# First RMSNorm of a decoder layer: sums of squares from a second, token-major load of x, and three weight tiles projected before the norm is known

## The chip, the core and the metric

The kernel runs on one core of a Trainium2 chip. A core has five engines with queues of their own: TensorE (PE, matmuls; PEld is its weight load), VectorE (DVE), ScalarE (ACT), GpSimd (POOL) and SyncE (SP, which here only issues DMAs and reads registers). The metric is the device time of one execution in microseconds (us), smaller is better. Of the kernel before there are three timed runs: 2433.55, 2440.73 and 2443.16 us, median 2440.73.

## The reference

One decoder layer with a hybrid mixer, for 512 prompt tokens and 32 sample tokens (8 sequences of 4) that share all weights, in float32. What matters here is its beginning:

```
def rmsnorm(x, w):
    y = x * rsqrt(mean(x * x, axis=-1) + EPS)       # mean over D_MODEL = 2048
    return y * w

h = rmsnorm(x, norm_mix_w)
proj = h @ w_in                                      # columns: q, k, v, z, xbc, dt_raw
xbc_c = silu(causal_dwconv(xbc, ...));  dt = softplus(dt_raw + dt_bias)
... attention, Mamba-2 scan, output projection, second norm, gated MLP, last norm
```

A token's factor rsqrt(...) multiplies a whole row of h, so it can be left out of the projection and multiplied into its result: proj = (x * w) @ w_in, times the factor of each token. Both kernels do that.

## The kernel before

**Layout.** Activations lie with features in partitions and tokens along the row: x comes as `xT`, 16 blocks (k = 0 to 15) of 128 features by 544 tokens, the tokens in two halves of 272 (256 prompt, 16 sample). Each float32 operand is split in two parts of lower precision, hi = rounded, lo = rest, and a product is three matmuls (hi x hi, hi x lo, lo x hi; `mm3`, L166). The split of weights is `wload` (L137): a DMA into `wraw`, ScalarE writes `whi` (L150), VectorE writes `wlo` (L151). An output tile of 128 columns of w_in is 2 halves x 16 k x 3 = 96 matmuls of 272 columns.

**First stage (L239 to L282).** For each k one DMA brings `xt`; `xh` is made by VectorE for even k (L251) and by ScalarE for odd k (L253), `xl` by VectorE (L254), times the norm's gain. ScalarE squares `xt` (L257, L260), and the squares are added up, three by VectorE, the others by GpSimd (L261), into `ssq`, which is a sum over k with features still in partitions. At the same time the weights of the first two output tiles (`FIRST`: columns 8 and 10 of the xbc part) come in pieces of 256 columns, and TensorE runs the 192 matmuls of both tiles as x arrives (L276). Amid them, after k = 13, `rms_rstd` (L207) sums `ssq` over the partitions with a matmul against ones (`pn`), which also spreads the sum over all partitions; ScalarE takes the square root (L213) and VectorE the reciprocal (L214) of 128 x 272 values for each half. The result is `rstd`.

**What follows.** The pool sA (`xt`, the first tiles' weights, the squares) is released and the pool sS takes its memory: what is first written in sS waits for the last reader in sA. `dt_linear` (L336) runs 64 matmuls for the columns of dt into PSUM (`podt`) with the weights `wdthi` (L274, L275). Then the tiles of xbc follow, each by `xbc` (L326): the matmuls of `linear`, then an evacuation that multiplies PSUM by `rstd` into `pre` (L305, L306), a convolution in `acc` (one ScalarE pass L314 and three VectorE passes L316), and a SiLU by ScalarE (L318, L319). The two first tiles have their matmuls behind them already, and go straight to the evacuation.

**What sets the order.** TensorE runs in the order in which the code is written. Small jobs (`dt_stage`, `lam`, `ssd`) are generators, which are polled between matmuls by a modelled clock (`side`), so that their matmuls are put between those of the tiles: `dt_stage` multiplies `podt` by `rstd` into `dtr` on VectorE (L347 to L349) and then transposes it by five small matmuls `pd` (L355). The order on the other engines is the scheduler's, by priority; it is fixed when the program is built, and each engine runs it in line.

**SP.** Its queue issues the loads of x and weights. After the first tile's weights 32 reads of the page table into registers stand in it (L631), ahead of all later weight loads. Three buffers hold `whi` and `wlo`, two hold `wraw`.

Of the kernel before, what the change touches and what calls it, by code (L numbers as in the profile page):

```python
# [16 lines left out]
P = 128  # L17
# [82 lines left out]
def body(tc, i, o):  # L100
# [12 lines left out]
    def rd(t):  # L113
        return t.bitcast(F32)
# [122 lines left out]
    fw = [[], []]  # L237
    sub = 256
    for k in range(NK):  # L239
        xt = sA.tile([P, 2, HT], F32, name="xt", tag="xt", bufs=6)  # L240
        dma(out=xt, in_=i["xT"][k])
        if k % 8 == 0:
            ch = [wload(i["w_in"][32 + j][:, k * P:k * P + WCH], sub, sA) for j in FIRST]
            for f in range(2):
                fw[f].append(ch[f][:2])
        if k % 2 == 0:
            for c in ch:
                c[2]((k % 8) // 2)
        xs[k] = xslot(k)
        if k % 2 == 0:  # L250
            V.tensor_scalar(xs[k][0], xt, nw_mix[:, k:k + 1], None, op0=ALU.mult)  # L251
        else:
            A.activation(xs[k][0], xt, AF.Copy, scale=nw_mix[:, k:k + 1])  # L253
        V.scalar_tensor_tensor(xs[k][1], xt, nw_mix[:, k:k + 1], rd(xs[k][0]), op0=ALU.mult, op1=ALU.subtract)  # L254
        e, acc = (V, ssq2) if k % 4 == 2 else (G, ssq)
        if k in (0, 2):
            A.activation(acc, xt, AF.Square)  # L257
        else:
            sq = sA.tile([P, 2, HT], F32, name="sq", tag="sq", bufs=3)
            A.activation(sq, xt, AF.Square)  # L260
            e.tensor_tensor(acc, acc, sq, op=ALU.add)  # L261
    k1 = pack(cst, "k1")
    ones, nw_ffn, nw_fin = (k1[n] for n in ("ones", "nw_ffn", "nw_fin"))
    V.tensor_tensor(ssq, ssq, ssq2, op=ALU.add)
    kS = pack(sC, "kS")
# [6 lines left out]
    wdt = kS["w_dt"].rearrange("p (k h) -> p k h", h=SH)  # L272
    whi = sC.tile([P, NK, 2 * SH], FR, name="wdthi")
    A.activation(whi[:, :, 0:SH], wdt, AF.Copy)  # L274
    V.tensor_tensor(whi[:, :, SH:2 * SH], wdt, rd(whi)[:, :, 0:SH], op=ALU.subtract)  # L275
    for k in range(NK):  # L276
        for f in range(2):
            for hf in range(2):
                mm3(first[f][hf], kslice(fw[f], k), xs[k], hf, k == 0, k == NK - 1)
        if k == 13:  # L280
            rstd = rms_rstd(cst, ssq, DM, tag="rstd")
    sA.release()  # L282
# [1150 lines left out]
def host_inputs(x):  # L1433
# [132 lines left out]
```

## Time and profile before

| | us |
|---|---|
| median of three runs | 2440.73 |
| the profiled execution's own time | 2442.75 |
| its span, first to last instruction | 2441.0 |
| TensorE busy | 2355.5 (96%) |
| VectorE busy | 2083.3 (85%) |
| ScalarE busy | 1141.7 (47%) |
| GpSimd busy | 722.6 (30%) |

The span and the own time differ by what lies before the first and after the last instruction. TensorE's clock has two levels, 1.2 and 2.4 GHz; the profile gives the granted share of the upper one, 0.986 as a mean of this execution. In the page's chain of waits 59% of the span is TensorE's. Times in rows count from the start of the span.

### The profile page before, as it was taken

The numbers are of one execution on the slowest core, as the hardware profiler recorded it, in microseconds if no ns is written. First come the engines' busy times: TensorE is split into PE (matmuls) and PEld (weight loads), VectorE is DVE, ScalarE is ACT, GpSimd is POOL, SyncE is SP. The second block draws the span as 40 slices with busy tenths as digits, with TensorE's granted clock in tenths as the row PEclk, the third lists the DMA queues.
The fourth block names the chain that finished last, engine by engine and source line by source line (L and its number), as shares of the span: only waits on it lengthen the run. The fifth ranks groups of instructions, "written<-read, shape, count | busy, mean of one in ns | idle before, by whom it ended". The sixth has DMA issues, their size and how long they took to land.

```text
span 2441.0 us, 46377 instructions
## 1 busy us (share of the span) xinstructions
PE 2355.5 (96%) x18184; PEld 2302.7 (94%) x18184; DVE 2083.3 (85%) x2893; ACT 1141.7 (47%) x1651; POOL 722.6 (30%) x655
## 2 busy tenths in 40 slices
PE   8999999999999999899999999999999899899997
PEld 7989898998999999899999999999999899898997
DVE  8686778787877556999999999999999988989986
ACT  5645345656565323444444444444444534435345
POOL 4243233333321113522222222322221222423223
PEclk9999999999999999899999999999999999999999
DMA  5434444444555443243434343333433755747432
GB/s 163 130 126 129 157 155 145 149 155 147 165 161 160 151 146 115 87 142 110 140 112 141 123 141 116 130 131 116 139 111 131 220 173 178 228 152 229 141 113 83
DMA packets 172285, 350.45 MB, mean 144 GB/s; under 512 B 19474, under 2 KB 89874, under 8 KB 172066
## 3 DMA queue, kind: packets, MB, share of 16 engines
q1 hardware_dynamic: 171250, 346.65, 44.1%
q8 instruction: 143, 2.34, 0.4%
q10 hardware_dynamic: 816, 0.84, 0.1%
q14 instruction: 76, 0.62, 0.1%
HBM read 293.07 MB, written 54.35 MB: 142 GB/s over the span
## 4 chain that ended last, share of the span: by engine, by line
PE 59%; DVE 7%; DMA 2%; issue 2%; ACT 1%; POOL 0%; DVEq 0%; SPq 0%; ACTq 0%; POOLq 0%
PE po L158 58%; DVE wlo L1062 2%; DVE xl L1062 1%; DMA st<-hTs 1%; DVE wx L1062 1%; ACT whi L1068 0%; DMA wraw<-in_w_gu 0%; DMA xr<-in_xT 0%; DVE ssq L1423 0%; DMA st<-hB 0%; PE pos L158 0%; PE scs L158 0%; ACT xh L1068 0%; DVE acc L316 0%; DMA wraw<-in_w_down 0%
## 5 line engine op out<-in xcount | busy, mean ns | idle before, releaser
L158 PE MATMUL po<-xh,whi 128*128 128x272 f32 x3968 | 1160.3, 292 | 18.4 <-ACT whi L150 5.2
L158 PE MATMUL po<-xh,wlo 128*128 128x272 f32 x3968 | 1152.6, 290 | 13.5 <-DVE wlo L1062 11.9
L158 PE MATMUL po<-xl,whi 128*128 128x272 f32 x3968 | 1150.1, 290 | 5.5 <-DVE xl L254 5.5
L158 PEld LDWEIGHTS po<-xh,whi 128*128 128x128 f32 x3968 | 756.4, 191 | 27.2 <-ACT whi L1068 8.0
L158 PEld LDWEIGHTS po<-xh,wlo 128*128 128x128 f32 x3968 | 754.8, 190 | 22.6 <-DVE wlo L1062 14.8
L158 PEld LDWEIGHTS po<-xl,whi 128*128 128x128 f32 x3968 | 755.3, 190 | 6.4 <-DVE xl L254 6.4
L1068 ACT ACTIVATE whi<-wx 128x1024 fp32r<-128x1024 f32 (+2 forms) x340 | 343.2, 1010 | 474.8 <-PE po L158 448.5
L1062 DVE TENSOR_TENSOR wlo<-wx,whi 128x1024 fp32r<-128x1024 f32 (+2 forms) x340 | 437.5, 1287 | 51.6 <-ACT whi L1068 49.4
L1068 ACT ACTIVATE whi<-wraw 128x1024 fp32r<-128x1024 f32 (+2 forms) x136 | 136.9, 1006 | 191.5 <-PE po L158 182.2
L151 DVE TENSOR_TENSOR wlo<-wraw,whi 128x1024 fp32r<-128x1024 f32 (+1 forms) x132 | 166.3, 1265 | 61.4 <-ACT whi L150 61.0
L1062 DVE TENSOR_TENSOR wlo<-wraw,whi 128x1024 fp32r<-128x1024 f32 (+2 forms) x136 | 170.6, 1254 | 7.4 <-ACT whi L1068 5.3
L1062 DVE TENSOR_TENSOR wx<-wraw,wx 128x1024 f32<-128x1024 f32 (+2 forms) x136 | 172.2, 1269 | 5.4 <-POOL wx L1062 2.9
L150 ACT ACTIVATE whi<-wraw 128x1024 fp32r<-128x1024 f32 (+1 forms) x132 | 127.8, 976 | 95.4 <-PE po L158 73.0
L699 POOL TENSOR_TENSOR kvl<-kv,kvh 128x512 fp32r<-128x512 f32 x64 | 105.0, 1641 | 178.4 <-ACT kvh L697 171.5
L158 PE MATMUL po<-T2h,whi 128*128 128x272 f32 x512 | 148.9, 291 | 5.3 <-DVE xr L1191 4.7
L158 PE MATMUL po<-B11h,whi 128*128 128x272 f32 x512 | 148.1, 289 | 5.7 <-DVE u L1136 5.7
L158 PE MATMUL po<-T2h,wlo 128*128 128x272 f32 x512 | 149.5, 292 | 3.3 <-DVE wlo L1062 3.3
L158 PE MATMUL po<-T2l,whi 128*128 128x272 f32 x512 | 149.2, 291 | 0.0
L158 PE MATMUL po<-T1h,wlo 128*128 128x272 f32 x512 | 147.7, 289 | 1.5 <-DVE wlo L1062 1.5
L158 PE MATMUL po<-B11h,wlo 128*128 128x272 f32 x512 | 148.3, 290 | 0.0
L158 PE MATMUL po<-B11l,whi 128*128 128x272 f32 x512 | 148.3, 290 | 0.0
L158 PE MATMUL po<-T1l,whi 128*128 128x272 f32 x512 | 147.5, 288 | 0.0
(406 smaller groups left out, 4196.4 us busy)
## 6 DMA issues: line engine op xcount, KB each, us to landing
wx<-in_w_gu SPq DMA_DIRECT2D x88, 512.0 KB, 3.9
wraw<-in_w_gu SPq DMA_DIRECT2D x88, 512.0 KB, 3.9
wraw<-in_w_in SPq DMA_DIRECT2D x84, 512.0 KB, 3.8
kv<-in_kc SPq DMA_DIRECT2D x128, 128.0 KB, 2.2
kv<-in_vc SPq DMA_DIRECT2D x128, 128.0 KB, 2.7
wraw<-in_w_out SPq DMA_DIRECT2D x32, 512.0 KB, 3.9
wx<-in_w_down SPq DMA_DIRECT2D x32, 448.0 KB, 3.6
wraw<-in_w_down SPq DMA_DIRECT2D x32, 448.0 KB, 3.6
```

Source lines behind the costliest of these rows:

```text
L150: A.activation(hi[:, c], raw[:, c], AF.Copy)
L151: V.tensor_tensor(lo[:, c], raw[:, c], rd(hi[:, c]), op=ALU.subtract)
L158: T.matmul(out, lhsT=lhsT, rhs=rhs, start=start, stop=stop)
L699: e.tensor_tensor(l[:, s], src[:, s], rd(h)[:, s], op=ALU.subtract)
L1062: e.tensor_tensor(out, a, b, op=op)
L1068: A.activation(h, src, AF.Copy)
```

## The change

- All sixteen `xh` are made by ScalarE; VectorE makes only `xl`. The squares, the adds on VectorE and GpSimd and `ssq` go.
- The sums of squares come from a second load of x, `xq`, now with tokens in partitions and features along the row: for each of 4 blocks of 128 prompt tokens two pieces of 128 x 1024, for the 32 sample tokens two of 32 x 1024. ScalarE issues these ten DMAs itself, and squares and sums each piece in one instruction with an accumulated output (`accum_out`) into a column of `ss`. Three buffers hold the pieces, so a load follows the sum that frees its buffer.
- `norm1` adds the two columns of each token, takes square root and reciprocal of 128 x 5 values, puts them on the diagonals of five matrices (`rdiag`), and spreads them over the partitions by six float32 matmuls against ones; ScalarE copies the result to `rstd`.
- The first two tiles leave PSUM without the factor, by four ScalarE copies into their later places `bc`; `xbc` then reads `bc` in place of PSUM. One more tile (column 0 of xbc, `held`) is run before `norm1` and waits in PSUM for the factor.
- The casts of `wdthi` and the loads of the next three weight pieces (`wfill`) stand after the first stage. ScalarE's order up to `norm1` is meant to be the written one (`manual_schedule`).

```diff
@@ first stage
+    act = contextlib.ExitStack()
+    act.enter_context(tc.manual_schedule(engines={mybir.EngineType.Activation}))
     for k in range(NK):
...
         xs[k] = xslot(k)
-        if k % 2 == 0:
-            V.tensor_scalar(xs[k][0], xt, nw_mix[:, k:k + 1], None, op0=ALU.mult)
-        else:
-            A.activation(xs[k][0], xt, AF.Copy, scale=nw_mix[:, k:k + 1])
+        A.activation(xs[k][0], xt, AF.Copy, scale=nw_mix[:, k:k + 1])
         V.scalar_tensor_tensor(xs[k][1], xt, nw_mix[:, k:k + 1], rd(xs[k][0]), op0=ALU.mult, op1=ALU.subtract)
-        e, acc = (V, ssq2) if k % 4 == 2 else (G, ssq)
-        if k in (0, 2):
-            A.activation(acc, xt, AF.Square)
-        else:
-            sq = sA.tile([P, 2, HT], F32, name="sq", tag="sq", bufs=3)
-            A.activation(sq, xt, AF.Square)
-            e.tensor_tensor(acc, acc, sq, op=ALU.add)
...
-    V.tensor_tensor(ssq, ssq, ssq2, op=ALU.add)
...
-        if k == 13:
-            rstd = rms_rstd(cst, ssq, DM, tag="rstd")
     sA.release()
@@ new, after the pool sS is allocated
+    def sq_load():
+        c, n = xq[len(xqs)]
+        t = sS.tile([P, 1024], F32, name="xq", tag="m", bufs=3)[:P if c < 4 else NS]
+        A.dma_start(out=t, in_=i["xtp"][c, :, n] if c < 4 else i["xts"][:, n])
+        xqs.append((t, ss[:P if c < 4 else NS, c, n:n + 1]))
+    def sq_sum(n, again):
+        t, acc = xqs[n]
+        A.activation(t, t, AF.Square, accum_out=acc)
+        if again:
+            sq_load()
+    wfill()
+    whi = sC.tile([P, NK, 2 * SH], FR, name="wdthi")
+    A.activation(whi[:, :, 0:SH], wdt, AF.Copy)
+    V.tensor_tensor(whi[:, :, SH:2 * SH], wdt, rd(whi)[:, :, 0:SH], op=ALU.subtract)
+    V.memset(ss[:, 4], 1.0)
+    for n in range(3):
+        sq_load()
+    for f in range(2):
+        for hf in range(2):
+            A.activation(bc[FIRST[f] - 8][:, hf], first[f][hf][:, 0:HT], AF.Copy)
+    for n in range(7):
+        sq_sum(n, True)
+    def norm1():
+        r = sS.tile([P, 5], F32, name="rcol")
+        V.tensor_tensor(r, ss[:, :, 0], ss[:, :, 1], op=ALU.add)
+        A.activation(r, r, AF.Sqrt, scale=1.0 / DM, bias=epsc)
+        V.reciprocal(r, r)
+        dg = sS.tile([P, 5, P], F32, name="rdiag", tag="m", bufs=3)
+        V.tensor_tensor(dg, ident.unsqueeze(1).broadcast_to([P, 5, P]), r.unsqueeze(2).broadcast_to([P, 5, P]), op=ALU.mult)
+        for hf in range(2):
+            pt = ps.tile([P, 512], F32, name="pn", tag=("sA", "pb")[hf])
+            for c in range(2):
+                mm(pt[:, c * P:(c + 1) * P], ones, dg[:, 2 * hf + c])
+            mm(pt[:, HP:HT], ones[:NS], dg[:NS, 4, hf * HS:(hf + 1) * HS])
+            A.activation(rstd[:, hf], pt[:, 0:HT], AF.Copy)
@@ after the first stage
     podt = dt_linear()
+    held = {0: []}
+    linear(xs, lambda hf, po: held[0].append(po))
+    for n in range(7, 10):
+        sq_sum(n, False)
+    norm1()
+    act.close()
...
-    for j in FIRST:
-        xbc(j)
-    for j in range(4):
+    for j in (0,) + FIRST + (1, 2, 3):
         xbc(j)
```

The built programs show what stands where. First ScalarE's queue at the end of the first stage, before (the numbers in tile names are buffers; `waits` names the engines and DMA lanes waited for):

```order
L150 ACTIVATE whi<-wraw 128x256 [waits DMAHW7_49]
L253 ACTIVATE xh_281<-xt,k_71 128x544 [waits DMAHW0_49]
L260 ACTIVATE sq<-xt 128x544 [waits Pool_49]
L274 ACTIVATE wdthi<-kS 128x16x16 [waits DMAHW2_49]
L213 ACT_TABLE_LOAD
L213 ACTIVATE rstd<-pn,k_71 128x272 [waits PE_49] x2
L150 ACTIVATE whi<-wraw 128x1024 [waits DMAHW5_49]
```

And the same place now, from the last block of x to the first sum (`ea` is a 16-wide tile of `dt_stage` in the pool sS, `bc` the copies of the first two tiles):

```order
L250 ACTIVATE xh_240<-xt,k_71 128x544 [waits DMAHW0_49]
L150 ACTIVATE whi<-wraw 128x1024 [waits DMAHW4_49]
L150 ACTIVATE whi<-wraw 128x1024 [waits DMAHW5_49]
L416 ACTIVATE ea<-kS 128x16 [waits DMAHW2_49,DVE_49,PE_49]
L150 ACTIVATE whi<-wraw 128x1024 [waits DMAHW7_49]
L294 ACTIVATE wdthi<-kS 128x16x16
L283 DMA xq<-in_xtp 128x1024 [waits DMAHW1_49]
L283 DMA xq<-in_xtp 128x1024
L283 DMA xq<-in_xtp 128x1024 [waits DMAHW3_49]
L301 ACTIVATE bc_449<-po 128x272 x2
L301 ACTIVATE bc_451<-po 128x272 x2
L288 ACTIVATE xq,ss<-xq 128x1024 [waits DMAHW1_49]
```

`wdthi`, which stood ahead of the norm, now stands behind `ea`, whose place in memory the first tiles' weights hold until their last matmul, and behind the third piece of weights.

ScalarE's queue further on, before `norm1` (with buffer numbers: `whi_576` is the second weight piece of the tile after `held`, `whi_1047` the first of the one after that):

```order
L283 DMA xq_502<-in_xts 32x1024 [waits Activation_49]
L288 ACTIVATE xq_496,ss_453<-xq_496 128x1024 [waits DMAHW0_49]
L283 DMA xq_505<-in_xts 32x1024 [waits Activation_49]
L150 ACTIVATE whi_576<-wraw_575 128x1024 [waits DVE_49,PE_49]
L288 ACTIVATE xq_499,ss_453<-xq_499 128x1024 [waits DMAHW1_49]
L288 ACTIVATE xq_502,ss_453<-xq_502 32x1024 [waits DMAHW2_49,DVE_49]
L288 ACTIVATE xq_505,ss_453<-xq_505 32x1024 [waits DMAHW3_49]
L150 ACTIVATE whi_1047<-wraw_1046 128x1024 [waits DMAHW7_49,DVE_49,PE_49]
L310 ACT_TABLE_LOAD
```

The last three sums stand behind `whi_576`, which takes the slot of the first weight piece of `held`: that is free when the second half of `held` has passed k = 7, which is 24 matmuls from its end. `whi_1047` takes the slot of the second piece, free at the end of `held`.

VectorE's queue from the evacuation to the operand of `pd` (`dtr`), before:

```order
L305 TENSOR_TENSOR pre<-po,rstd 128x256
L306 TENSOR_TENSOR pre<-po,rstd 128x4x4
L151 TENSOR_TENSOR wlo<-wraw,whi 128x1024
L316 SCALAR_TENSOR_TENSOR acc<-pre,kS,acc 128x568 x6
L151 TENSOR_TENSOR wlo<-wraw,whi 128x1024
L347 TENSOR_TENSOR dtr<-podt,rstd 32x512
L348 TENSOR_TENSOR dtr<-podt,rstd 32x32
```

And now:

```order
L336 TENSOR_TENSOR pre<-bc_449,rstd 128x256
L337 TENSOR_TENSOR pre<-bc_449,rstd 128x4x4
L347 SCALAR_TENSOR_TENSOR acc<-pre,kS,acc 128x568 x6
L336 TENSOR_TENSOR pre<-bc_451,rstd 128x256
L337 TENSOR_TENSOR pre<-bc_451,rstd 128x4x4
L336 TENSOR_TENSOR pre<-bc_451,rstd 128x256
L337 TENSOR_TENSOR pre<-bc_451,rstd 128x4x4
L347 SCALAR_TENSOR_TENSOR acc<-pre,kS,acc 128x568 x3
L381 TENSOR_TENSOR dtr<-podt,rstd 32x512
L382 TENSOR_TENSOR dtr<-podt,rstd 32x32
L580 CAST cm<-bss 128x8x4
L383 COPY dtr<-dtr 32x64
```

`dtr` stood behind two tiles' evacuation and convolution, and stands behind three. On TensorE the five matmuls `pd` stand 36 matmuls after the start of column 0's tile before, and 36 matmuls after the start of column 1's tile now, which is the first one behind `norm1`.

## Rows read from the trace of the kernel before

**Rows 1.** Stretches: start and end, length, each engine's busy time, TensorE's granted clock, DMA.

```profile
5.00:10.00 5.00, 4.62 (x18) 4.15 (x19) 3.47 (x6) 3.31 (x8) 1.37 (x1) 1.00 0.98 329
...
35.00:40.00 5.00, 3.34 (x19) 3.35 (x20) 5.00 (x8) 1.44 (x2) 1.02 (x1) 0.79 0.20 64
...
38.00:41.00 3.00, 3.00 (x14) 2.67 (x12) 3.00 (x7) 0.00 (x0) 0.00 (x0) 0.50 0.56 146
```

**Rows 2.** VectorE's groups, 0 to 45 us, and the tile xt: min/median/max ns.

```profile
L254 DVE SCALAR_TENSOR_TENSOR xl<-xt,k,xh x16: 769/779/1918, 4.8 to 39.6; 128x544 fp32r<-128x544 f32 x16
...
L151 DVE TENSOR_TENSOR wlo<-wraw,whi 128x256 fp32r<-128x256 f32 x16 | 10.6, 704 | 0.1
...
L251 DVE TENSOR_SCALAR xh<-xt,k 128x544 fp32r<-128x544 f32 x8 | 6.2, 772 | 5.7 <-DMA xt<-in_xT 5.7
...
L261 DVE TENSOR_TENSOR ssqb<-ssqb,sq 128x544 f32<-128x544 f32 x3 | 2.1, 712 | 0.0
```

**Rows 3.** GpSimd's group of adds, 0 to 45 us: busy, mean ns, idle before.

```profile
L261 POOL TENSOR_TENSOR ssq<-ssq,sq 128x544 f32<-128x544 f32 x11 | 16.8, 1525 | 18.8 <-ACT sq L260 17.8 <-DMA kS<-in_kS 0.5
```

**Rows 4.** TensorE in order of time: start, duration, what.

```profile
5.20 0.59 PE L158 MATMUL po<-xh,whi 128*128 128x272 f32 x1 [5.20 <-ACT whi L150]
...
7.50 0.43 PE L158 MATMUL po<-xh,wlo 128*128 128x272 f32 x1
7.73 0.43 PE L158 MATMUL po<-xl,whi 128*128 128x272 f32 x1
...
10.64 0.29 PE L158 MATMUL po<-xl,whi 128*128 128x272 f32 x1
```

**Rows 5.** The matmuls podt, pd and pn: duration, first and last start.

```profile
L158 PE MATMUL podt<-xh,wdthi x32: 282/287/292, 45.2 to 52.8; 128*32 128x272 f32 x32
...
L158 PE MATMUL pd<-kS,dtr x10: 231/257/278, 57.7 to 58.7; 32*128 32x16 f32 x8, 32*96 32x16 f32 x2
...
L158 PE MATMUL pn<-ssq,k 128*128 128x272 f32 x4 | 1.3, 443 | 0.1
```

**Rows 6.** ScalarE's groups, 0 to 45 us.

```profile
L150 ACT ACTIVATE whi<-wraw 128x256 fp32r<-128x256 f32 x16 | 6.1, 407 | 1.8 <-DMA wraw<-in_w_in 1.6
L253 ACT ACTIVATE xh<-xt,k 128x544 fp32r<-128x544 f32 x8 | 5.9, 742 | 5.9 <-DMA xt<-in_xT 5.9
L150 ACT ACTIVATE whi<-wraw 128x1024 fp32r<-128x1024 f32 x2 | 2.0, 1047 | 0.0
...
L213 ACT ACT_TABLE_LOAD x1 | 1.3, 1283 | 0.0
...
L213 ACT ACTIVATE rstd<-pn,k 128x272 f32<-128x272 f32 x2 | 0.9, 488 | 5.5 <-PE pn L158 5.5
```

**Rows 7.** ScalarE in order of time, the second tile's first weight piece.

```profile
5.58 0.42 ACT L150 ACTIVATE whi<-wraw 128x256 fp32r<-128x256 f32 x1 [0.44 <-DMA wraw<-in_w_in]
```

**Rows 8.** DMAs of the first 75 us: KB each, median us from issue to landing.

```profile
wraw<-in_w_in SPq DMA_DIRECT2D x7, 512.0 KB, 3.9
...
kT<-in_kT SPq DMA_DIRECT2D x1, 764.5 KB, 6.8
```

**Rows 9.** The attention's accumulated exponentials: the read of the accumulator.

```profile
L784 ACT ACTIVATION_READ_ACCUMULATOR p<-sc,mx x64: 189/196/208, 336.2 to 723.7; 128x1 f32 x64
```

**Rows 10.** VectorE in order of time, from the first evacuation to dtr.

```profile
45.96 0.36 DVE L305 TENSOR_TENSOR pre<-po,rstd 128x256 f32<-128x256 f32 x1
...
48.69 5.51 DVE L316 SCALAR_TENSOR_TENSOR acc<-pre,kS,acc 128x568 f32<-128x568 f32 x6
54.12 1.21 DVE L151 TENSOR_TENSOR wlo<-wraw,whi 128x1024 fp32r<-128x1024 f32 x1
55.26 0.67 DVE L347 TENSOR_TENSOR dtr<-podt,rstd 32x512 f32<-32x512 f32 x1
```

**Rows 11.** SP's reads of the page table: duration, first and last start.

```profile
L631 SPq TENSOR_LOAD <-ptab x32: 262/262/481, 38.9 to 57.2; - x32
```

**Rows 12.** What TensorE waited for from 45 to 170 us: us, times, longest.

```profile
PE py L158 <- DVE mixy L504: 0.5, 1, 0.5
```

More of the change, by code (lines that the diff above doesn't have):

```diff
@@ L224, in body @@
     xs = {}
-    ssq = sA.tile([P, 2, HT], F32, name="ssq")
-    ssq2 = sA.tile([P, 2, HT], F32, name="ssqb")
     first = [[half(), half()], [half(), half("sB")]]
@@ L272, in body @@
     wdt = kS["w_dt"].rearrange("p (k h) -> p k h", h=SH)
-    whi = sC.tile([P, NK, 2 * SH], FR, name="wdthi")
-    A.activation(whi[:, :, 0:SH], wdt, AF.Copy)
-    V.tensor_tensor(whi[:, :, SH:2 * SH], wdt, rd(whi)[:, :, 0:SH], op=ALU.subtract)
     for k in range(NK):
@@ L289, in body @@
     bc = [sS.tile([P, 2, HT], F32, name=f"bc{j}") for j in range(4)]
+    ss = sS.tile([P, 5, 2], F32, name="ss")
+    xq = [(c, n) for c in range(5) for n in range(2)]
+    xqs = []
+    def sq_load():
[20 more added lines that the diff above has]
+        sq_sum(n, True)
+    rstd = cst.tile([P, 2, HT], F32, name="rstd", tag="rstd")
+    def norm1():
[11 more added lines that the diff above has]
+            A.activation(rstd[:, hf], pt[:, 0:HT], AF.Copy)
     def conv(pool, tg, lin, nw, par, prev, tail, dst, bufs=2):
@@ L330, in xbc @@
             for hf in range(2):
-                evac(hf, first[FIRST.index(j)][hf])
+                evac(hf, dst[:, hf])
+        elif j in held:
+            for hf in range(2):
+                evac(hf, held[j][hf])
         else:
@@ L1440, in host_inputs @@
     d["xT"] = xx.T.reshape(NK, P, 2, HT)
+    d["xtp"] = np.asarray(x["x_prompt"]).reshape(4, P, 2, DM // 2)
+    d["xts"] = np.asarray(x["x_sample"]).reshape(NS, 2, DM // 2)
     w_in = np.asarray(x["w_in"])[0]
```

## Prediction

> **What bounds the kernel now.** I read the page's busy shares first: TensorE is busy 96% of the span, so a change at the start counts only by how much sooner or later TensorE gets through its queue. Then the stretches of the first 60 us, TensorE's waits, VectorE's groups, and last the instructions in order of time around the norm. The reader is to see two things. In the first stage TensorE starves behind VectorE: from 35 to 40 us VectorE is busy 5.00 of 5, TensorE 3.34, and its granted clock falls to 0.50, the lower of its two levels, from 38 to 41 us [rows 1]. VectorE is slow because its instructions stretch: `xl` takes 779 ns as a median but up to 1918, and the 256-wide `wlo` 704 ns as a mean [rows 2], beside eleven adds of 1525 ns on GpSimd [rows 3]. Behind the first stage TensorE has no idle time worth naming: 0.5 us from 45 to 170 us [rows 12]. So whatever the change gains or loses up to the matmuls `pd` goes into the time almost in full. I follow TensorE to the end of `pd`, in both kernels.
>
> **Before.** `dt_linear` starts at 45.2 us and its 62nd of 64 matmuls at 52.8 (the list has those that read `xh`, two of every four), so a matmul takes (52.8 - 45.2)/61 = 0.125 us at the upper level. The last `pd` starts at 58.7 and ends about 58.9 [rows 5].
>
> **The first stage.** Removed from VectorE: eight `xh` (6.2 us) and three adds (2.1) [rows 2]; from GpSimd everything (16.8) [rows 3]. VectorE keeps 16 x 0.779 + 16 x 0.704 = 23.7 us, even with the stretched `wlo`; ScalarE has 16 x 0.742 + 16 x 0.407 = 18.4 us [rows 6]. Sixteen times 272 KB of x and 16 x 128 KB of weights are 6.55 MB, 20 us at the 329 GB/s of 5 to 10 us [rows 1]. All three are below TensorE's own 192 matmuls, so TensorE becomes the bound. It starts later: `xh` of k = 0 now stands behind the second tile's weight piece, which ends at 5.58 + 0.42 = 6.00 [rows 7]; plus 0.74 [rows 6] the first matmul comes at 6.74 instead of 5.20 [rows 4], and the third waits 0.35 more for `xl`. Today the first matmuls run 0.227 us apart (7.50 to 7.73), until about 10.64, 5.4 us after the start [rows 4]. If that is so again, (5.4 - 0.35)/0.227 = 22 matmuls are done by 12.1, and 170 x 0.125 = 21.2 us later the stage ends: 33.3 us against 45.2, a gain of 11.9. The bounds: all at the upper level, 7.1 + 192 x 0.125 = 31.1; a stage that starves and runs half its matmuls at the lower level, 33.3 + 96 x 0.102 = 43.
>
> Behind this stands a rule. The trace shows `xl` at 779 ns and at 1918 [rows 2]. The Trainium skill (SBUF — State Buffer, Who interferes with whom) says that a VectorE instruction with two SBUF inputs and a GpSimd instruction that reads SBUF exclude each other for a whole instruction. The stretched rows agree. The rule also speaks against the change: the evacuations from `bc` now have two SBUF inputs, beside GpSimd's two multiplies of the cosine and sine tables; by it the chain below would be up to 2 x 1.5 = 3 us longer. The sum is made without that.
>
> **dt_linear starts late.** After the last matmul ScalarE runs `ea` (about 0.2, as small an instruction as the accumulator read of [rows 9]), a weight piece (1.05) and the cast of `wdthi` (0.41) [rows 6]. VectorE has a 1024-wide `wlo` (1.21) [rows 10] between, and then the low part of `wdthi` (0.4 to 0.7, as the 256-wide `wlo`). With 0.3 us for the last matmul to end: 33.3 + 0.3 + 0.2 + 1.05 + 1.21 + 0.5 = 36.5. TensorE idles 3.2 us where it idled none. The bounds are 0, if nothing were in the way, and 4 with a late weight load.
>
> **Two tiles' worth at one go.** 64 + 96 matmuls take 160 x 0.125 = 20.0 us, to 56.5. After today's idle time the clock was at 0.50 for 3 us at least [rows 1], which costs 3 x (1 - 0.125/0.227) = 1.3 us; by the 5.4 us of the start it is 2.4. I take 2.0: column 0's tile ends at 58.5, bounds 56.5 and 59.
>
> **The norm.** Seven sums run beside TensorE. The last three wait in ScalarE's line behind `whi_576`, whose slot is free 24 matmuls before the tile's end, at 58.5 - 3.0 = 55.5. From there, each in turn: weight piece 1.05; three sums of 1.05 + 0.20 (the wide cast [rows 6] and the accumulator's read [rows 9]; the sample pieces are as long per partition) = 3.75; `whi_1047` 1.05; a table load 1.28; square root 0.2; reciprocal 0.2; the diagonals of 128 x 640, by the 712 ns of 544 columns [rows 2], 0.84. That is 8.4 us: 63.9. TensorE idles 5.4 us. The six matmuls together have the 2 x 272 float32 columns of today's `pn`, 1.3 us [rows 5], half of it before the first copy (0.49 [rows 6]): `rstd` stands at 63.9 + 0.65 + 0.49 = 65.0. Nothing hides this wait, since it begins with a slot that TensorE itself frees and TensorE's next work is `pn`. The load ahead of `whi_1047` is queued behind the 32 page-table reads, which take 18.9 us [rows 11], but these start some 20 us earlier than needed.
>
> The trace has a table load at 1283 ns [rows 6]. The Trainium skill (ScalarE: Activation LUTs, Rules for kernel authors) budgets about 2.7 us for a switch; by it the norm would be 1.4 us later. The row decides.
>
> **The new wait at pd.** From the first evacuation to `dtr` it is 55.26 - 45.96 = 9.3 us today [rows 10], with two `wlo` of 1.21, so 6.9 for two tiles. The third tile adds half of that, 3.45, and ScalarE's first pass, which nothing covers now (about 0.74, as `xh`); the second half of `rstd` comes 0.4 late. `dtr` starts at 65.0 + 6.9 + 4.2 + 0.4 = 76.5. Behind it stand 0.84 of its own and a cast that now waits for the SiLU of the third tile and GpSimd's copies of it, together about 2.0 until the last operand. With the last matmuls `pd` is over at about 78.9. TensorE gets there at 63.9 + 1.3 + 36 x (0.125 to 0.227) = 69.7 to 73.4: 5 to 9 us idle. Behind the waiting `pd` the rest of column 1's tile is queued, and all that follows. The bounds are 0, if VectorE had done `dtr` first, and 10.
>
> **The sum.** Before, `pd` was over at 58.9, with 96 matmuls fewer done: 58.9 + 96 x 0.125 = 70.9. Now 78.9, so 8.0 us later, and a third stretch at the lower level behind that idle time, 2.0: about 10 us lost. In short: 11.9 gained; 3.2 + 2.0 + 5.4 + 1.3 (today's `pn` lies inside the first stage) lost ahead of the norm's result, some 8 at `pd`, 2.0 after. From its own time of 2442.75 the profiled execution would go to 2452.7. The median of the runs lies 2.0 below it, so I predict 2451 us.
>
> **Rivals.**
> - *The gain is kept (faster).* Place: the two waits of TensorE at `pn` and `pd`. If the sums are over when column 0's tile ends and `dtr` is there in time, only 3.2 + 2.0 + 1.3 of 11.9 is lost: 5.4 us gained, 2435. It decides below 70.9 - 58.5 = 12.4 us from the end of that tile to the end of `pd`; I count 20.4. For it: ScalarE is free to run seven sums early. Against it: the order, in which three sums and nine convolution passes stand ahead. Chance 0.05, 0.03 of it beyond 0.5%, where the wait ahead of `podt` and the lower level go too.
> - *Part of it.* The stage ends at 31.1, no stretch at the lower level, the chain to `dtr` 1.5 us shorter: 10 - 2.2 - 4 - 1.5 = 2 us later, 2443. Chance 0.08.
> - *The second load comes late (slower by more).* Ten loads share three buffers. A load of 512 KB takes 3.9 us alone [rows 8]; with the sum and the issue a round of three is about 5.5 us, so seven sums from about 39 us end near 52, 3 us ahead of 55.5. With rounds of 8.5 (764 KB took 6.8 [rows 8]) they end near 58 and the norm is 3 to 5 us later: 2455. Against it: beside them only the weights of one more tile are loaded. Chance 0.22.
> - *The first stage does not get faster as it should (the change doesn't do what it says).* Every `xl` waits for ScalarE now, and each break in TensorE's work may bring the lower level: at 43 us instead of 33.3, 2461; at 36, 2454. Chance 0.12.
>
> **How the numbers follow.** What I forecast, a loss of 4 to 12 us, has 0.53. A difference of 0.5%, 12.2 us, is about what a measurement here can tell from no change. Faster by more than that: 0.03. Slower by more: the two late rivals where they pass 2453, and the upper end of my own terms, 0.36. Within: 0.61. The range leaves out the kept gain below and the worst first stage above: 2440 to 2461.
>
> **What would show it.** Right: `dt_linear` starts near 36 us, TensorE idles about 3, 5 and 7 us ahead of `podt`, `pn` and `pd`, the sums' last three run after 55, and no GpSimd work lies in the first 40 us. Wrong: `pd` over before 70 us, or a loss that later stretches give back; then the order on VectorE or the gain of the first stage was misjudged.

## The result and the profile after

The changed kernel takes 2456.32 us as the median of five runs (2454.61 to 2459.76), the kernel before 2440.73 beside it: ratio 1.0072, 95% interval 1.0055 to 1.0088. That is 15.6 us lost, against 10 in the forecast; it lies inside the range, and on the side "slower by over 0.5%", which had a chance of 0.36 against 0.61 for "within". The profiled execution spans 2457.5 us at a mean clock of 0.982 (before 2441.0 and 0.986).

What TensorE waited for in the first 200 us after (us in all, times, longest us) answers to [rows 12], where there was 0.5 us from 45 to 170 us:

```profile
PE po L158 <- ACT xh L250: 7.3, 1, 7.3
PE podt L158 <- DVE wdthi L295: 6.8, 1, 6.8
PE pd L158 <- ACT bc L350: 6.3, 1, 6.3
PE pn L158 <- issue: 5.0, 1, 5.0
PE pys L158 <- DVE h0l L597: 3.5, 3, 2.2
```

The first row is the start of the kernel. The next three are the waits the prediction named, 18.1 us together. The same stretches by windows (length, busy time and count of PE, PEld, DVE, ACT, POOL, granted clock, DMA share, GB/s) answer to [rows 1]:

```profile
10.00:15.00 5.00, 5.00 (x37) 5.00 (x36) 4.97 (x10) 4.73 (x9) 0.00 (x0) 1.00 0.95 330
25.00:30.00 5.00, 5.00 (x42) 5.00 (x42) 2.78 (x5) 2.03 (x4) 0.00 (x0) 1.00 0.99 330
30.00:35.00 5.00, 3.45 (x28) 3.24 (x27) 1.96 (x7) 2.22 (x3) 1.49 (x4) 1.00 0.34 134
35.00:40.00 5.00, 0.00 (x0) 0.00 (x0) 2.17 (x3) 2.15 (x5) 1.30 (x2) 0.86 0.68 247
40.00:45.00 5.00, 4.80 (x22) 3.61 (x23) 0.15 (x1) 2.05 (x5) 0.00 (x0) 0.50 0.79 279
65.00:70.00 5.00, 2.41 (x9) 2.18 (x10) 2.28 (x4) 1.79 (x3) 0.00 (x0) 0.59 0.29 105
80.00:85.00 5.00, 0.64 (x4) 0.67 (x4) 3.61 (x8) 2.33 (x4) 0.87 (x5) 0.79 0.00 0
85.00:90.00 5.00, 5.00 (x24) 4.96 (x25) 2.05 (x9) 0.83 (x2) 0.25 (x2) 0.52 0.00 0
```

From the first matmul at 7.3 us to 33.5 TensorE runs without a break, and GpSimd has nothing to do from 0.5 us to 33.5; then come three holes, and behind each a stretch at the lower level (0.50 from 40 to 45 us, 0.52 from 85 to 90, and 0.59 for a window from 65 to 70 that has part of a hole in it), where about half as many matmuls are done in 5 us. VectorE's groups of the first 45 us have lost their tails, against [rows 2] (busy, mean ns, idle before):

```profile
L251 DVE SCALAR_TENSOR_TENSOR xl<-xt,k,xh 128x544 fp32r<-128x544 f32 x16 | 12.0, 781 | 1.8 <-ACT xh L250 1.5
L151 DVE TENSOR_TENSOR wlo<-wraw,whi 128x256 fp32r<-128x256 f32 x16 | 6.3, 421 | 8.2 <-ACT whi L150 8.2
```

The loss shows whole at the scan: its matmuls `py` run 17.4 to 17.6 us later (duration, first and last start; before, then after).

```profile
L158 PE MATMUL py<-m,xdt x128: 272/273/323, 126.7 to 255.2; 128*64 128x128 f32 x128
```
```profile
L158 PE MATMUL py<-m,xdt x128: 272/273/324, 144.1 to 272.8; 128*64 128x128 f32 x128
```

### The profile page after: what moved, and what is told of

It is laid out like the page before. It is cut to its first block, busy times and chain, and to the rows that moved or that the text cites. A ratio compares the mean times of both kernels' runs of the same rounds, so it can differ in the third digit from the quotient of the medians.

```text
span 2457.5 us, 46389 instructions
## 1 busy us (share of the span) xinstructions
PE 2359.4 (96%) x18192; PEld 2307.6 (94%) x18192; DVE 2065.3 (84%) x2883; ACT 1147.9 (47%) x1667; POOL 701.6 (29%) x644
## 5 line engine op out<-in xcount | busy, mean ns | idle before, releaser
L158 PE MATMUL po<-xh,wlo 128*128 128x272 f32 x3968 | 1152.7, 290 | 13.4 <-DVE wlo L1100 12.0
L151 DVE TENSOR_TENSOR wlo<-wraw,whi 128x1024 fp32r<-128x1024 f32 (+1 forms) x132 | 159.6, 1212 | 93.4 <-ACT whi L150 93.1
L150 ACT ACTIVATE whi<-wraw 128x1024 fp32r<-128x1024 f32 (+1 forms) x132 | 127.6, 975 | 103.0 <-PE po L158 75.4
```

The lines of the kernel that those rows point to most:

```text
L150: A.activation(hi[:, c], raw[:, c], AF.Copy)
L151: V.tensor_tensor(lo[:, c], raw[:, c], rd(hi[:, c]), op=ALU.subtract)
L158: T.matmul(out, lhsT=lhsT, rhs=rhs, start=start, stop=stop)
```

## The experiments

Twelve kernels. The runs of one kernel scatter by 2 to 13 us, the places in a trace by less, so both are given. How much less can be read from four traces whose code is the same up to `pn` (the changed kernel, `e2`, `e6`, `e10`): there `pn` starts between 65.3 and 67.6. In the table, `podt`, `pn`, `pd` and `py` are first starts, the last column is the last start of `py<-m`. From there to the median time it is 2181 to 2189 us in every row, the two kernels too: what a version gains or loses is there when the scan ends.

| kernel | median us | ratio to before, 95% | podt | pn | pd | py | last py |
|---|---|---|---|---|---|---|---|
| before | 2440.3 | | 45.2 | | 57.7 | 126.7 | 255.2 |
| after | 2456.3 | 1.0055 to 1.0088 | 40.2 | 67.6 | 84.4 | 144.1 | 272.8 |
| e4_before_no_pool | 2429.4 | 0.9939 to 0.9964 | 33.4 | | 45.9 | 114.9 | 244.1 |
| e12_xh_act | 2440.0 | 0.9989 to 1.0006 | 42.8 | | 55.4 | 124.3 | 252.6 |
| e9_sums_on_pe | 2430.7 | 0.9944 to 0.9975 | 35.4 | | 48.1 | 117.0 | 246.9 |
| e1_wdt_first | 2453.9 | 1.0036 to 1.0062 | 33.0 | 66.5 | 83.3 | 143.8 | 273.2 |
| e3_sums_early | 2456.2 | 1.0054 to 1.0078 | 40.7 | 65.2 | 80.8 | 140.9 | 267.7 |
| e2_dtr_first | 2454.5 | 1.0043 to 1.0069 | 40.4 | 67.6 | 75.4 | 141.2 | 269.8 |
| e7_three | 2449.7 | 1.0031 to 1.0057 | 33.1 | 64.5 | 71.2 | 138.4 | 267.3 |
| e5_load_first | 2458.0 | 1.0060 to 1.0085 | 33.3 | 67.2 | 83.9 | 143.8 | 270.3 |
| e6_pool_late | 2457.2 | 1.0053 to 1.0079 | 39.9 | 66.5 | 83.3 | 144.2 | 274.3 |
| e10_no_mult | 2456.0 | 1.0055 to 1.0081 | 38.6 | 65.3 | 80.4 | 140.5 | 269.5 |
| e8_two_held | 2443.2 | 0.9999 to 1.0021 | 31.7 | 71.8 | 76.1 | 140.0 | 258.0 |
| e11_two_held_b | 2441.2 | 0.9994 to 1.0015 | 33.8 | 65.7 | 70.0 | 134.8 | 255.5 |

**Where the first stage's gain comes from.** In the kernel before, GpSimd's adds alone were left out:

```diff
-            e.tensor_tensor(acc, acc, sq, op=ALU.add)
+            if e is V:
+                e.tensor_tensor(acc, acc, sq, op=ALU.add)
```

> The kernel before the change, with GpSimd's eleven adds of the squares left out (so its sum of squares lacks them); ScalarE still squares, VectorE still makes eight `xh` and three adds. It asks whether the 11.7 us that the first stage gained come from GpSimd's adds alone or also from moving `xh` to ScalarE. Theory (VectorE was slow because it shared with GpSimd): `xl` back to 0.78 us without a tail, `wlo` to 0.42, so VectorE needs some 29 us for this stage, TensorE is the bound, and the stage ends near 35 instead of 45.2: 2431 to 2432 against 2440.7. Rival (VectorE's own work was the bound): the stage ends above 40, 2436 or more.

`podt` starts at 33.4, 11.8 us sooner, and nearly all of it stays: 2429.4, 10.7 us less than the kernel before beside it (2440.0). In the trace VectorE's `xh` too is faster, 500 ns as a mean against 772 [rows 2]:

```profile
L254 DVE SCALAR_TENSOR_TENSOR xl<-xt,k,xh 128x544 fp32r<-128x544 f32 x16 | 12.1, 782 | 0.1
L151 DVE TENSOR_TENSOR wlo<-wraw,whi 128x256 fp32r<-128x256 f32 x16 | 6.1, 422 | 1.0 <-ACT whi L150 1.0
L251 DVE TENSOR_SCALAR xh<-xt,k 128x544 fp32r<-128x544 f32 x8 | 4.0, 500 | 5.2 <-DMA xt<-in_xT 5.2
```

So the gain that the change makes in its first stage needs neither the second load nor ScalarE's sixteen `xh`, only that GpSimd doesn't add. The other half, in the kernel before:

```diff
-        if k % 2 == 0:
-            V.tensor_scalar(xs[k][0], xt, nw_mix[:, k:k + 1], None, op0=ALU.mult)
-        else:
-            A.activation(xs[k][0], xt, AF.Copy, scale=nw_mix[:, k:k + 1])
+        A.activation(xs[k][0], xt, AF.Copy, scale=nw_mix[:, k:k + 1])
```

> The kernel before the change with all sixteen `xh` on ScalarE, GpSimd's and VectorE's adds as they were: the other half of what the change does to the first stage. Theory (the adds are what slows VectorE): VectorE loses 6.2 us of work but stays stretched, the first stage ends above 40 and `podt` starts 2 to 4 us sooner than 45.2: 2437. Rival (VectorE's load as such): `podt` below 37, 2431.

The place is the theory's: `podt` 2.4 us sooner. The time is not: 2437 was expected, and the 2440.0 measured can't be told from the kernel before (0.9989 to 1.0006). VectorE has 6.2 us less to do, but beside the eleven adds its instructions stay stretched:

```profile
L251 DVE SCALAR_TENSOR_TENSOR xl<-xt,k,xh 128x544 fp32r<-128x544 f32 x16 | 18.7, 1186 | 6.7 <-ACT xh L250 6.7
L151 DVE TENSOR_TENSOR wlo<-wraw,whi 128x256 fp32r<-128x256 f32 x16 | 10.5, 696 | 0.1
```

**The three waits, one by one.** The casts of `wdthi` were put back ahead of the first stage's matmuls:

```diff
     wdt = kS["w_dt"].rearrange("p (k h) -> p k h", h=SH)
+    whi = sC.tile([P, NK, 2 * SH], FR, name="wdthi")
+    A.activation(whi[:, :, 0:SH], wdt, AF.Copy)
+    V.tensor_tensor(whi[:, :, SH:2 * SH], wdt, rd(whi)[:, :, 0:SH], op=ALU.subtract)
...
     wfill()
-    whi = sC.tile([P, NK, 2 * SH], FR, name="wdthi")
...
```

> The changed kernel with one thing moved: the two casts that make `wdthi` stand ahead of the first stage's matmuls, as before the change, no longer behind `ea` and the third weight piece. Theory (three waits in a row, of which the later ones take up slack): the 6.8 us of TensorE ahead of `podt` shrink to under 1 and the lower clock of 40 to 45 us goes, so column 0's tile ends near 54 instead of 62.6; but the seventh sum now decides instead of TensorE's slot (it ended at 56.3, perhaps 55 now), so `pn` comes near 63 instead of 67.6 and TensorE's wait there grows from 5.0 to 8 or 9: 4 to 5 us of 2456.3 come back, 2452. Rival A (each wait counts by itself): 8 to 9 us come back, 2448. Rival B (the chain of sums and norm sets the end of this part whatever TensorE does ahead of it): nothing comes back, 2456.

Nearly nothing comes back: `py` moves by 0.3 us, which is rival B. The wait ahead of `podt` is gone, and the one at `pn` has grown from 5.0 to 13.4:

```profile
PE pn L158 <- issue: 13.4, 1, 13.4
PE pd L158 <- ACT bc L350: 7.1, 1, 7.1
```

The theory was too hopeful by 3.5 us at `pn`: in this trace the seventh sum ends at 56.3, as it did after, and the ninth waits 1.67 us more for its load. In the changed kernel TensorE's gate (59.7) and the loads (the seventh sum at 56.3, three sums to go) were almost equally late, so that taking away either one shows the other. The wait at `pn` takes up what TensorE wins ahead of it.

The last three sums ahead of the gated weight piece:

```diff
     for n in range(7):
         sq_sum(n, True)
+    for n in range(7, 10):
+        sq_sum(n, False)
...
     linear(xs, lambda hf, po: held[0].append(po))
-    for n in range(7, 10):
-        sq_sum(n, False)
```

> The changed kernel with the last three sums (and only they) ahead of the weight piece that TensorE's slot gates. Theory: that piece is gated by TensorE at 59.7 and the sums are over by about 60, so the 3.2 us that the sums cost behind it go: `pn` near 64.5 instead of 67.6, 2453. Rival (the second load is late and decides): the sums wait for their loads, `pn` does not move by more than 1 us, 2456.

The trace follows the theory: `pn` 2.4 us sooner, and TensorE's wait there 1.9 us, where it is 5.0 in all four traces named above. From `podt` to `pn` it is 24.5 us, where it is 26.6 to 27.4 in those four. `py` is 3.2 us sooner. The median of six runs, 2456.2 (2452.14 to 2461.3), does not show it.

`dtr` first on VectorE:

```diff
     t_dt = side.add(dt_stage(podt, res))
+    for n in range(2):
+        side._next(t_dt)
```

> The changed kernel with one thing moved: `dt_stage` is taken up to its operand `dtr` right after `norm1`, so that on VectorE `dtr` stands ahead of the three evacuations and convolutions; `pd` stands 18 matmuls into column 1's tile instead of 36. Theory: `dtr` is ready near 73, TensorE reaches `pd` near 74, so the 6.3 us wait and the lower clock of 85 to 90 us behind it go: 6 to 8 us come back, 2449. Rival (the wait only moves on, to the evacuations of column 1 and 2 or to the scan, which now come about 1.5 us later): less than 2 us come back, 2455.

The wait at `pd` is gone and `pd` comes 9.0 us sooner, but `py` only 2.9. The wait has moved along the chain: TensorE stops 3.1 us at `pc`, the next matmul that needs dt, since the series of dt now stands among the convolutions on VectorE, and the lower clock comes behind it (0.67 from 100 to 110 us). The rival was nearer than the theory.

All three together:

> The first three experiments in one kernel: casts of `wdthi` early, ten sums ahead of the gated weight piece, `dtr` first on VectorE; the weight pieces and the loads in the changed kernel's order. Theory (the chain from the second load on sets the time): loads issued at 36.4 as in the first experiment, tenth sum 23.4 us later at 59.8, `pn` near 63.6 against 67.6; TensorE waits some 9 to 10 us at `pn`, not at `pd`; the scan's first matmul `py` comes 4.0 + 2.9 (what the second experiment gave) = 7 us sooner, near 137, and 2449. Rival (what each gave adds up by itself): `py` near 144.1 - 0.3 - 2.9 - 3.2 = 137.7, the same time, but then TensorE's wait at `pn` is under 3 us. Second rival (the load is late whatever the order): `pn` above 65, 2453.

`pn` at 64.5, `py` at 138.4, 2449.7 us, close to the theory's 63.6, 137 and 2449; and TensorE waits 11.3 us at `pn`, which only the theory says. The three edits work on one chain, not on three waits:

```profile
PE pn L158 <- issue: 11.3, 1, 11.3
PE po L158 <- ACT xh L250: 6.5, 1, 6.5
PE pc L158 <- DVE dta L420: 3.1, 1, 3.1
```

**The second load.** Beside the first and third experiment's edits, the first three loads were issued ahead of the weight pieces:

```diff
-    wfill()
...
     for n in range(3):
         sq_load()
+    wfill()
```

> The changed kernel with ScalarE's order alone altered, at three places: the casts of `wdthi` ahead of the first stage's end (as in the first experiment), the last three sums ahead of the gated weight piece (as in the third), and the first three loads of the second copy of x ahead of the three weight pieces, so that they are issued at the end of the first stage, near 33.7, and not at 36 to 38. Theory (from `podt` on the chain load, ten sums, norm, evacuation, `dtr`, `pd` sets the time, not TensorE's own work): the tenth sum ended 23.4 us after the first load's issue in the third experiment, so it ends at 57.1, and `pn` starts near 61 instead of 67.6, although TensorE now gets there at 53.5 and waits 7: the scan's first matmul `py` comes 6 to 7 us sooner than 144.1, and 2450 us. Rival (beside the weights the loads only take longer): the tenth sum stays above 60, `pn` above 64, 2453 or more.

It failed. The rival's numbers came (`pn` at 67.2, 2458), but the loads of x were not what was late. They go out at 33.5, but now the third weight piece comes late, and the copies that free PSUM and all the sums stand behind it on ScalarE (start, duration, idle before):

```profile
33.52 1.36 ACTq L286 DMA_DIRECT2D xq<-in_xtp  x3
34.93 2.01 ACT L150 ACTIVATE whi<-wraw 128x1024 fp32r<-128x1024 f32 x2 [6.48 <-issue]
...
43.98 1.06 ACT L150 ACTIVATE whi<-wraw 128x1024 fp32r<-128x1024 f32 x1 [6.94 <-DMA wraw<-in_w_in]
44.94 1.24 ACT L301 ACTIVATE bc<-po 128x272 f32<-128x272 f32 x4
46.05 1.08 ACT L291 ACTIVATE xq<-xq 128x1024 f32<-128x1024 f32 x1
```

Four microseconds of queue were saved (the loads went out at 37.5 after the change) and seven of waiting put in their place. The weight piece itself needed only 3.1 us from issue to landing. Its load was issued late: VectorE had freed the buffer by 37.2, but in this order 15 of the 32 reads of the page table stand ahead of the load on SP, and they run from 31.6 to 40.3. In the changed kernel the same load goes out before the reads, which start at 36.2 there. SP's queue, the changed kernel first:

```profile
34.51 1.60 SPq L149 DMA_DIRECT2D wraw<-in_w_in  x2
```
```profile
40.89 10.85 SPq L149 DMA_DIRECT2D wraw<-in_w_in  x3
```

**GpSimd's two multiplies behind the norm.** They were moved in the code to behind the convolutions' tiles:

```diff
-    G.tensor_tensor(cosr, cosr, rstd, op=ALU.mult)
-    G.tensor_tensor(sinr, sinr, rstd, op=ALU.mult)
...
     dma(out=o["tail_ssd"], in_=ctail)
+    G.tensor_tensor(cosr, cosr, rstd, op=ALU.mult)
+    G.tensor_tensor(sinr, sinr, rstd, op=ALU.mult)
```

> The changed kernel with GpSimd's two multiplies of the cosine and sine tables moved behind the convolutions' tiles, out of the stretch right behind `rstd`; nothing else. Theory (these two hold up VectorE's evacuations from SBUF, 1.25 and 1.33 us where 0.42 and 0.17 are usual): `pre` from `bc` is 0.42 and 0.17 throughout, `dtr` and `pd` come 2.0 us sooner (`pd` at 82.4 instead of 84.4), `py` at 142, 2454. Rival (the evacuations are slow because they read `bc` beside ScalarE's or a DMA's writes): they stay above 1 us and nothing moves.

This tested nothing: the scheduler put them at the same place in GpSimd's queue, in the trace they start at 70.5 with the second copy of `rstd`, and VectorE shows the same 1.25 and 1.32 us. It serves as a second trace of the changed kernel, and shows how far two traces of one order differ: `pn` 1.1 us, `py` 0.1, the last `py` 1.5. So they were left out instead:

> The changed kernel without GpSimd's two multiplies of the cosine and sine tables by `rstd` (left out, so the rotary embedding lacks the norm's factor). In the sixth experiment the edit left GpSimd's queue as it was, so it showed nothing of this. Theory (the two multiplies hold up VectorE's evacuations from SBUF): `pre` from `bc` takes 0.42 and 0.17 us in the second half too, not 1.25 and 1.33; `dtr` comes 2.0 us nearer behind `rstd` (12.1 instead of 14.2 from the first copy of `rstd`), `py` near 142, 2454. Rival (it is the read of `bc` itself): unchanged.

The slow pair is now like the others (start, duration):

```profile
69.61 0.41 DVE L336 TENSOR_TENSOR pre<-bc,rstd 128x256 f32<-128x256 f32 x1
69.95 0.18 DVE L337 TENSOR_TENSOR pre<-bc,rstd 128x16 f32<-128x16 f32 x1
```

From the first evacuation to `dtr` it is 12.15 us (67.50 to 79.65) instead of 13.80 (69.78 to 83.58); from the first copy of `rstd`, as the expectation counted, 12.6 instead of 14.2, where 12.1 was expected. So 1.65 us is what the two multiplies cost on the chain. The time does not show it: the median is 2456.0. `py` comes 3.6 us sooner; the rest of that goes with the earlier start of `pn` in this execution (65.3), whose wait ahead of `podt` was 5.2; with the code the same up to there it was 6.8, 7.3, 7.1 and 5.9 in four other traces.

**Keeping the gain.** A version with two tiles ahead of the norm, core of the edit:

```diff
+    held = {1: []}
+    def keep(hf, po):
+        A.activation(mixy[0][:, 0, hf], po[:, 0:HT], AF.Copy)
+    linear(xs, keep)
     for n in range(7, 10):
         sq_sum(n, False)
-    norm1()
+    dg = norm1()
+    linear(xs, lambda hf, po: held[1].append(po))
+    norm2(dg)
...
+        with tc.high_priority(offset=120):
...
```

> A version meant to keep what the first stage gained. To the changed kernel: casts of `wdthi` and loads of the second copy of x as in the fifth experiment; two tiles (columns 0 and 1) run ahead of the norm's matmuls instead of one, column 0 copied out of PSUM by ScalarE; the norm's square root and diagonals stand before the second of them; `dtr` first on VectorE behind the norm, the series of dt raised in priority; GpSimd's two multiplies late. Theory (work that needs no norm must last as long as the chain to the norm): TensorE gets to `pn` at 33.5 + 8 + 24 = 65.5, the diagonals are there near 62, so no wait above 1 us at `podt`, `pn` and `pd`, no stretch at the lower clock from 30 to 90 us, and the 11.7 us of the first stage are kept but for `pn` and some waits in the scan: 2431 to 2434. Rival (VectorE's four convolutions and the dt series behind the norm become the bound): TensorE waits 5 us or more at `pc` or at the evacuations, and it is 2438 or more.

No wait at `pn` and `pd`, and 13 us better than the changed kernel, but not the forecast: the third weight piece was late here too (its load was issued at 40.9, behind the same 15 reads, and its cast began at 44.07), with 5.7 us of TensorE's time at 41 us, and `pc` waited 3.3. (GpSimd's two multiplies stayed right behind `rstd` here too, and in the next one.) Mended:

```diff
+    for n in range(2):
+        wbuf.append(next(wseq[0]))
-    wfill()
...
         sq_sum(n, True)
+        if n == 3:
+            wfill()
...
-        yield 16.0
+        yield 22.0
```

> The eighth experiment's kernel (two tiles ahead of the norm) with the third weight piece moved on ScalarE behind the fourth sum, so that the copies which free PSUM and the sums no longer wait for its load (44 us there), and with `pc` asked for 6 us later. Theory: the 5.7 us wait at 41 us goes with the lower clock behind it, `pn` starts near 65.5 without a wait, `pc` waits less than 1 us, and what the first stage gained is kept but for 2 to 3 us: 2433 to 2436 against 2443. Rival (VectorE is the bound behind the norm, busy 5.00 of 5 from 80 to 95 us there): the waits move to `pys` and to the evacuations, 2440 or more.

No wait from 33 to 120 us is over 1.3 us, the clock stays at 1.00, and the time is still that of the kernel before. What TensorE waits for from 33 to 330 us shows where the gain went:

```profile
PE po L158 <- DVE q L760: 6.8, 1, 6.8
PE pys L158 <- DVE h0l L604: 3.9, 4, 2.5
```

`q` is the attention's first tile. Its place in memory is the scan's, which is free only when the scan's outputs are written (VectorE in order of time):

```profile
296.77 0.72 DVE L634 SCALAR_TENSOR_TENSOR mixy<-xss,kS,pys 128x32 f32<-128x32 f32 x4 [7.53 <-PE pys L158]
297.41 3.56 DVE L214 RECIPROCAL rstd<-rstd 128x272 f32<-128x272 f32 x2
...
302.68 2.87 DVE L658 SCALAR_TENSOR_TENSOR mixy<-mixy,kT,rstd 128x544 f32<-128x544 f32 x4
...
309.70 0.79 DVE L760 COPY q<-po 128x272 f32<-128x272 f32 x2 [3.01 <-DMA mixd<-mixy]
```

The rival's 2440 or more was right; its reason, VectorE as the bound, is not shown. The place is the end of the scan, where VectorE had itself waited 7.5 us for `pys`. With `rstd` at 67 us (46 in the kernel before) the scan's last `py` starts at 255.5, no sooner than in the kernel before. TensorE had run ahead of the scan and waits there. Counted in matmuls, it is 84 ahead of the kernel before at 100 us (714 against 630), 51 at 256, and none at 330 (2348 against 2349). So of 11.4 us gained at `podt`, about 1.7 went to `pn`, 3.2 to idle time from 100 to 256 us (6.9 us of it, against 3.7 before), and 6.8 is paid back at `q`. Why the scan ends no sooner, by VectorE's work or by the places of its matmuls in TensorE's written order, no run separates.

**The short way.** From the kernel before, with the squares summed by TensorE:

```diff
-        e, acc = (V, ssq2) if k % 4 == 2 else (G, ssq)
...
+        sqs[k] = sA.tile([P, 2, HT], FR, name="sq", tag="sq", bufs=5)
+        A.activation(sqs[k], xt, AF.Square)
...
+        for hf in range(2):
+            mm(pn[hf][:, 0:HT], one_r, sqs[k][:, hf], k == 0, k == NK - 1)
```

> Another way to the same end, from the kernel before: no second load, nothing reordered; ScalarE writes the squares in the type of the split operands, and TensorE sums them over k and partitions at once, 32 matmuls of 272 columns against ones in the first stage, so that the fourteen adds on GpSimd and VectorE and the four float32 `pn` go. Theory (the adds beside VectorE's splits were the whole loss, as the fourth experiment showed by 10.7 us): the first stage is bound by TensorE and ends as there plus 32 x 0.125 - 1.3 = 2.7 us, 2432 to 2433. Rival (five buffers of squares tie ScalarE to TensorE's pace and the weights' casts wait behind the squares): TensorE breaks off and shows the lower clock within the first stage, 2437 or more.

2430.7 us: faster than both kernels, ratio to before 0.9959 (0.9944 to 0.9975). The whole first stage in one window:

```profile
5.00:35.00 30.00, 29.63 (x221) 29.32 (x222) 22.29 (x44) 21.95 (x43) 0.00 (x0) 1.00 0.83 284
```

TensorE is busy 29.63 of 30, at the upper level throughout; VectorE and ScalarE have a quarter of their time left. The price of 32 more matmuls was worked out as 2.7 us; `podt` at 35.4 is 2.0 behind the run without GpSimd's adds. The squares are rounded once to the split operands' type.

## Why the prediction was right, and which terms were off

The order of events was as forecast at every step, and the time fell into the range. The loss was forecast too small, 10 us against 15.6. Times of the steps, us:

| step | forecast | measured | behind by |
|---|---|---|---|
| first stage ends | 33.3 | 33.5 | 0.2 |
| `podt` starts | 36.5 | 40.2 | 3.7 |
| column 0's tile ends | 58.5 | 62.6 | 4.1 |
| `whi_576` | 55.5 | 59.7 | 4.2 |
| `pn` starts | 63.9 | 67.6 | 3.7 |
| `rstd` | 65.0 | 69.7 | 4.7 |
| `dtr` | 76.5 | 83.6 | 7.1 |
| `pd` over | 78.9 | 86.5 | 7.6 |

- *First stage.* Right, with some luck: two errors cancelled. The first matmul came at 7.32 instead of 6.74, but the slow matmuls behind it lasted only to 11.2 instead of 12.1. So 22 had started by 12.0, where 22 by 12.1 had been forecast.
- *dt_linear starts late.* This term failed: 6.8 us of idle time, outside the bounds of 0 to 4. I gave the third weight piece 1.05 us, its cast. ScalarE's row shows that its load was late:

```profile
34.34 0.20 ACT L416 ACTIVATE ea<-kS 128x16 f32<-128x16 f32 x1
37.50 1.06 ACT L150 ACTIVATE whi<-wraw 128x1024 fp32r<-128x1024 f32 x1 [2.96 <-DMA wraw<-in_w_in]
...
38.46 0.40 ACT L294 ACTIVATE wdthi<-kS 128x256 fp32r<-128x256 f32 x1
```

  Two buffers hold `wraw`, so this load could go out only when VectorE had made the first piece's `wlo` (34.5), and that piece had itself landed late, behind the two packs. A weight piece that is cast "next" is not yet loaded. It was the largest error in the forecast, and yet worth 0.3 us at `py`, as the first experiment shows, because the loads of the rival "the second load comes late" stood right behind it. That rival, priced at 2455, was the hidden bound. The first sum started 5.5 us after its load was issued (37.5 to 43.0), and the two rounds of three behind it took 5.2 and 7.0 us, where I had 5.5 for each; so the seventh sum ended at 56.3 where I had it at 52.
  "Nothing hides this wait" was wrong for the same reason, and so was the sum's list of losses, which adds the waits up: in the first experiment the wait ahead of `podt` is gone and `pn` starts at 66.5 all the same, 2.6 us behind the forecast. TensorE's waits mark where the chain from the second load to `pd` holds it up; they are not losses to be added.
- *Two tiles, the norm.* 22.4 us for 22.0, and 7.9 from `whi_576` to `pn` for 8.4, TensorE idle 5.0 for 5.4. The last three sums stand where the order had them:

```profile
56.32 0.32 ACTq L283 DMA_DIRECT2D xq<-in_xts  x1
59.67 1.06 ACT L150 ACTIVATE whi<-wraw 128x1024 fp32r<-128x1024 f32 x1 [3.38 <-PE po L158]
60.63 1.05 ACT L288 ACTIVATE xq<-xq 128x1024 f32<-128x1024 f32 x1
...
66.10 0.30 ACT L310 ACTIVATE rcol<-rcol,k 128x5 f32<-128x5 f32 x1
69.35 0.40 ACT L319 ACTIVATE rstd<-pn 128x272 f32<-128x272 f32 x1 [2.95 <-PE pn L158]
```

- *pn.* Mis-sized. I took 1.3 us at the upper level; behind the wait it ran at the lower one (granted clock 0.50 from 67 to 70 us), 370 to 582 ns each, and 3.0 us from first to last start. With 1.9 us of wait ahead (third experiment) it was 257 to 389 ns:

```profile
L158 PE MATMUL pn<-rdiag,k x12: 370/421/582, 67.6 to 70.6; 128*128 128x128 f32 x8, 32*128 32x16 f32 x4
```
```profile
L158 PE MATMUL pn<-rdiag,k x12: 257/275/389, 65.2 to 67.0; 128*128 128x128 f32 x8, 32*128 32x16 f32 x4
```

- *The chain to dtr.* 13.8 us from the first evacuation, 11.5 forecast from `rstd`. 1.65 of the 2.3 us between them is GpSimd's two multiplies, which the prediction had named beside the sum and left out:

```profile
71.47 0.42 DVE L336 TENSOR_TENSOR pre<-po,rstd 128x256 f32<-128x256 f32 x1 [0.76 <-ACT rstd L319]
...
71.89 1.25 DVE L336 TENSOR_TENSOR pre<-bc,rstd 128x256 f32<-128x256 f32 x1
73.06 1.33 DVE L337 TENSOR_TENSOR pre<-bc,rstd 128x16 f32<-128x16 f32 x1
...
83.58 0.68 DVE L381 TENSOR_TENSOR dtr<-podt,rstd 32x512 f32<-32x512 f32 x1
```

  The evacuation from PSUM has one input in SBUF and took 0.42; the two from `bc` have two. The Trainium skill (SBUF — State Buffer, Who interferes with whom) says that a VectorE instruction with two SBUF inputs and a GpSimd instruction that reads SBUF exclude each other for a whole instruction. The rows agree, and the tenth experiment shows it; the estimate by it in the prediction was 3 us at most.
- *The sum.* I set the loss as 8.0 + 2.0. At the end of `pd` it was 86.5 - 70.9 = 15.6. The lower clock behind `pd` (0.52) is there as forecast, and at `py` the loss is 17.4, so some 2 us do come on top. Whether the time has them the runs can't tell: the medians differ by 15.6, the two profiled executions by 16.6, and the ratio 1.0072 stands for 17.6.
- *Signs.* Of those named, the last three sums ran after 55 us, and the waits were 6.8, 5.0 and 6.3 us for 3, 5 and 7. `dt_linear` did not start near 36 us, and GpSimd was not empty for 40 us: it set and copied some small tiles from 33.5 to 36.3.
- *Rivals.* The kept gain did not come about, and the eleventh experiment says why: with every wait near the norm gone the time is only that of the kernel before. The first stage did get faster.

## What to carry to other kernels

When a chain to a result is made longer and TensorE is filled up with work that does not need the result, count the chain to its end (here the scan, 200 us on) and not TensorE's idle time alone: two tiles ahead of the norm took away every wait nearby, and the time came out as before. Ask first which of a change's parts makes its gain, by a run that leaves that part alone out; here GpSimd's adds were all of it, and a dozen lines give the gain without the chain. Before a cast is put in front of something urgent, look when its load can be issued (here a buffer held it, and in `e5_load_first` 15 reads on SP as well), not only how long the cast is.

## What the runs showed of the hardware

- VectorE's `xh`, with one tensor input in SBUF, took 772 ns as a mean beside GpSimd's adds and 500 without them (fourth experiment); `xl` had means of 1121 and 782.
- Behind TensorE's breaks at `podt` (6.8 us), `pn` (5.0) and `pd` (6.3) in the changed kernel the matmuls ran at the lower clock level from the first one on. Behind two shorter breaks the level fell only after the work had begun again. At `pn` in the third experiment (1.9 us, work again from 65.2) `pn` still ran at its upper durations, and the granted clock is 1.00 from 65 to 66 us and 0.50 from 67 to 70; at `pc` in the second (3.1 us, work again from 97.9) it is 1.00 from 97 to 99 us and 0.50 from 100 to 105.
- The changed kernel's first 15 matmuls, behind 7.3 us without any, started 0.227 us apart and more, as at the lower level (7.32 to 11.02 us), and yet the profile gives a granted clock of 1.00 there (layout as in the windows above):

```profile
5.00:10.00 5.00, 2.68 (x10) 2.37 (x11) 3.20 (x6) 3.23 (x8) 0.00 (x0) 1.00 0.99 331
```

- The wait ahead of `podt`, set by a weight load, was 5.2 to 7.3 us over five traces with the same code up to there.
- ScalarE's squares written in the split operands' type took 643 ns as a mean for 128 x 544 (ninth experiment), as those written in float32 did in the kernel before.
